# The first MLP product as Strassen's seven block products, with weight sums formed by accumulating DMA transfers

## The chip, the core and the metric

The kernel runs on one core of a Trainium2 chip. The metric is device time in microseconds, the median of several executions. A second number, the span, is the time from the first to the last instruction of one profiled execution; the rows further down come from that execution.

## The reference

Two decoder layers over 256 tokens of 2048 features. Each has a token mixer (differential attention in layer 0, dilated attention in layer 1), four heads that attend to 256 memory tokens, an output projection, and an MLP with 8192 hidden features. All in float32.

```
for i in range(DEPTH):                       # DEPTH = 2
    h = _rmsnorm(x, g_attn[i])
    proj = h @ w_in[i]                       # q, k, v, qm
    ...
    x = x + merged @ w_out[i]
    hm = _rmsnorm(x, g_mlp[i])
    x = x + jnp.square(jax.nn.relu(hm @ w_mlp1[i])) @ w_mlp2[i]
return _rmsnorm(x, g_final)
```

`w_mlp1` is 2048 x 8192, `w_mlp2` is 8192 x 2048. The change touches `hm @ w_mlp1[i]`.

## The kernel before

**Products.** A float32 number is held as two parts, hi and lo, in the type that TensorE takes at full rate; a product is hi x hi + hi x lo + lo x hi. Weights come from DRAM as float32 into a tile `raw`; `split` makes the parts: ScalarE copies to hi (line 108), VectorE subtracts to get lo (line 109). There are three raw tiles of 2048 columns, and four hi and four lo tiles of 1024.

**Two forms of matrix product.** `gemm_feat` (lines 124 to 151) keeps the weights stationary: per row tile of 128 and per block of 128 output features one matmul of 512 columns, hi weights against hi and lo activations side by side (line 142), and one of 256 columns, lo weights against hi activations (line 139). `gemm_tok_piece` (lines 153 to 163) keeps the tokens stationary, with three matmuls of 512 columns per row tile and token block (lines 161 to 163).

**The MLP.** It runs over 8 chunks of 1024 hidden features in each layer. `mlp_up(c)` does four `gemm_feat` with 2048 rows each (PSUM tile ps_u, weights hi_u and lo_u), adds the two halves (fb_u on line 214, ft_u on 216), squares the positive part (usq, line 540) and splits it into the tiles hT, hidden features by tokens. `mlp_down(c)` does four column blocks of 512 (PSUM tile psd, weights hi_d and lo_d), and adds each to x with the factor 1/rms^2 (line 562). The program is written as up(0), then for every c up(c+1), down(c).

**What sets the order.** The tile framework sorts the instructions when the program is built and fixes one list per engine; an engine takes its list in order. Two PSUM tiles of two banks (tag mm) hold what `gemm_feat` and the token form add up, four tiles of one bank (tag at) the rest. GpSimd does a few small operations and issues no transfer; loads are issued by SyncE.

```
split(hi, lo, raw[:, h * 1024:(h + 1) * 1024])
high(start=(k == 0), stop=False)
low(start=False, stop=False)
```

Of the kernel before, what the change touches and what calls it, by code (L numbers as in the profile page):

```python
# [9 lines left out]
F32 = mybir.dt.float32  # L10
F32R = mybir.dt.float32r
# [21 lines left out]
TMP = 6  # L33
GROUPS = ((128, 1), (512, 4), (2048, 16))
# [17 lines left out]
def trunk(ctx: ExitStack, tc: tile.TileContext, x, mem, g_attn, w_in, w_out, lambda_qk,  # L52
# [6 lines left out]
    apool = ctx.enter_context(tc.tile_pool(name="apool", bufs=8))  # L59
# [6 lines left out]
    x_sb = const.tile([P, 2, D], F32, name="x_sb")  # L66

    def load_weights(src, k, c, nm, parts=1):
        raw = wpool.tile([P, 2048], F32, tag="raw", name=f"raw_{nm}")
        n = k // parts  # L70
        for h in range(parts):
            yield nc.sync.dma_start(
                raw[:, h * n * c:(h + 1) * n * c].rearrange("p (k c) -> p k c", c=c),
                src[h * n * P:(h + 1) * n * P, :].rearrange("(k p) c -> p k c", p=P))
        yield raw
# [3 lines left out]
    first = [load_weights(w_in[0][pc * 1024:(pc + 1) * 1024, 3 * MIXW:3 * MIXW + 256], 8, 256, f"qm00_{pc}", 2)  # L79
             for pc in range(2)]  # L80
    for c in range(4):
        sl = slice(c * 512, (c + 1) * 512)
        nc.sync.dma_start(x_sb[:, :, sl], x[0].rearrange("(t p) d -> p t d", p=P)[:, :, sl])
        next(first[c // 2])
    first_raw = [next(f) for f in first]

# [6 lines left out]
    # matmuls on zeros that bring the tensor engine to its full clock while the first loads run  # L93
    zero = const.tile([P, 512], BF16, name="zero")
# [16 lines left out]
    def weights(src, k, c, nm, raw=None):  # L111
        """k row tiles of c columns, k * c = 2048, as two (hi, lo) pairs of k/2 row tiles."""
        if raw is None:
            *_, raw = load_weights(src, k, c, nm)
        res = []
        for h in range(2):
            hi = wpool.tile([P, 1024], F32R, tag="whi", bufs=4, name=f"hi_{nm}_{h}")
            lo = wpool.tile([P, 1024], F32R, tag="wlo", bufs=4, name=f"lo_{nm}_{h}")
            split(hi, lo, raw[:, h * 1024:(h + 1) * 1024])
            for kk in range(k // 2):  # L120
                res.append((hi[:, kk * c:(kk + 1) * c], lo[:, kk * c:(kk + 1) * c]))
        return res

    def gemm_feat(w, acts, nm, raws=(None, None)):
        """[256 features, 256 tokens] as [128, 2, 2, 256]: the two halves of dim 2 add up."""
        ps = pmm.tile([P, 2, 512], F32, tag="mm", name=f"ps_{nm}")
        k0 = 0
        for pc in range(2):
            wt = weights(w[pc * 1024:(pc + 1) * 1024, :], 8, 256, f"{nm}_{pc}", raws[pc])
            for kk in range(8):  # L130
                k = k0 + kk
# [18 lines left out]
            k0 += 8  # L150
        return ps.rearrange("p j (h t) -> p j h t", h=2)

    def gemm_tok_piece(ps, w, acts4, first, last, nm):
        """adds w[512, 512] against four activation tiles into ps [128, 2 token blocks, 512]."""
        wt = weights(w, 4, 512, nm)
        for kk in range(4):
            hi, lo = wt[kk]
# [10 lines left out]
    def to_feat(src_of_tok, c, dst, gcol, nm):  # L168
        """tokens x 512 features (chunk c) -> features x tokens times g, split into dst."""
# [14 lines left out]

    def sumsq(src, acc):
        junk = work.tile([P, 512], F32, tag="ev", bufs=EV, name="junk")
        nc.scalar.activation(junk[:, :src.shape[-1]], src, AF.Square, accum_out=acc)
# [6 lines left out]
    def rstd_of(ssq, nm):  # L194
        """ssq [128, 2, 4] -> 1 / rms by token [128, 2]."""
# [6 lines left out]
    def bcast_row(r, nm):  # L202
        """[128, 2] by token -> [128, 256], the tokens along the free axis in every partition."""
# [7 lines left out]
    def feat_sum(ps, nm):  # L211
        """the two halves of a gemm_feat result added: [128, 2, 256] in SBUF."""
# [20 lines left out]
    kmT = const.tile([P, DEPTH, NM, S], F32, name="kmT")  # L233
    vm = const.tile([P, DEPTH, 2, MEMW], F32, name="vm")
    memT = []
    mssq = small.tile([P, 2, 4], F32, tag="ssq", name="mssq")

    def load_mem(hf):
        m_t = wpool.tile([P, 2, 1024], F32, tag="raw", name=f"mem{hf}")
        nc.sync.dma_start(m_t, mem[0].rearrange("(t p) d -> p t d", p=P)[:, :, hf * 1024:(hf + 1) * 1024])  # L240
        for cc in range(2):
            c = 2 * hf + cc
            mt = act_tile(f"memT{c}")
            to_feat(lambda t: m_t[:, t, :], cc, mt, 4 * KT + 4 * (c - cc), f"mem{c}")
            memT.append(mt)
            for t in range(2):
                sumsq(m_t[:, t, cc * 512:(cc + 1) * 512], mssq[:, t, c:c + 1])

    def project_mem():
        mrstd = rstd_of(mssq, "mem")  # L250
        mrowb = bcast_row(mrstd, "mem")
        for i in range(DEPTH):
            for c in range(2):
                ps = gemm_feat(w_mem_kv[i][:, c * 256:(c + 1) * 256], memT, f"km{i}{c}")
                feat_scaled(kmT[:, i, 2 * c:2 * c + 2, :], ps, 1.0, mrowb, f"km{i}{c}")
# [4 lines left out]
            for t in range(2):  # L260
                nc.scalar.activation(vm[:, i, t, :], ps[:, t, :], AF.Copy, scale=mrstd[:, t:t + 1])

# [61 lines left out]
    def mem_head(i, h, qT, dst):  # L324
        """one memory head; dst [128, 2, 256] takes its output, features x tokens, split."""
        nm = f"m{i}{h}"
        sc = pat.tile([P, 2, S], F32, tag="at", name=f"sc_{nm}")
        for q in range(2):
            nc.tensor.matmul(sc[:, q, :], qT[:, q * P:(q + 1) * P], kmT[:, i, h, :], start=True, stop=True)
# [17 lines left out]
        for kb in range(2):  # L347
            nc.tensor.matmul(o[:, :S], vm[:, i, kb, h * HD:(h + 1) * HD], pT[:, kb, :],
# [301 lines left out]
```

## Time and profile before

| | us |
|---|---|
| median of 3 runs | 2239.72 |
| lowest, highest | 2239.68, 2239.79 |
| span of the profiled execution | 2237.8 |

The time of the profiled execution is not listed apart from its span; the span stands 1.9 us below the median. Of the span, TensorE is busy for 2226.3 us, VectorE for 1335.5, ScalarE for 1040.7, GpSimd for 14.0. The page of the profile gives such totals, the chain of work that ended last, groups of instructions by line (ps_u is the PSUM tile of the first MLP product, psd that of the second), and DMA issues with the time from issue to landing. Numbers behind a tile's name are buffer numbers.

### The profile page before, as it was taken

To read this page: it belongs to the slowest core of one execution; us is meant where nothing else is said; L and a number is where in the kernel's file an instruction comes from. 1 tells how busy PE (TensorE), PEld (TensorE's weight loads), DVE (VectorE), ACT (ScalarE), POOL (GpSimd) and SP (SyncE) were. 2 spreads that over 40 slices of the span, in tenths; PEclk is the share of its full clock that TensorE was granted. 3 is DMA by queue.
4 is the path that set the end of the run, shared out by engine and by line. 5 is a ranking of instruction groups with operands and counts; after the bars stand their busy time and mean duration, and the time that the engine had idled before them with its cause. 6 is when DMAs were issued, how large, how long until landed. Compare 5 with 4: busy or idle time off the path is not lost.

```text
span 2237.8 us, 27970 instructions
## 1 busy us (share of the span) xinstructions
PE 2226.3 (99%) x11462; PEld 1885.6 (84%) x11462; DVE 1335.5 (60%) x1568; ACT 1040.7 (47%) x1362; POOL 14.0 (1%) x26
## 2 busy tenths in 40 slices
PE   9999999999999999999999999999999999999998
PEld 7888878888888888888888888888888888888887
DVE  7557765565555555555666665555656555555555
ACT  7445554544344444444455544454444444434443
POOL 0000000000000000000000000000000000000000
PEclk9999999999999999999999999999999999999999
DMA  8554454566656656666555455456665665665664
GB/s 266 189 178 161 151 169 162 177 187 188 190 188 188 193 186 192 192 189 193 191 187 166 156 170 188 151 188 188 188 189 188 188 188 190 187 195 188 188 203 148
DMA packets 304849, 411.96 MB, mean 184 GB/s; under 512 B 6529, under 2 KB 203346, under 8 KB 304722
## 3 DMA queue, kind: packets, MB, share of 16 engines
q1 hardware_dynamic: 304448, 410.02, 57.7%
q8 instruction: 89, 1.46, 0.3%
q14 instruction: 38, 0.31, 0.0%
q10 hardware_dynamic: 274, 0.17, 0.0%
HBM read 408.07 MB, written 2.10 MB: 183 GB/s over the span
## 4 chain that ended last, share of the span: by engine, by line
PE 98%; DMA 1%; ACT 0%; issue 0%; DVE 0%; SPq 0%; POOL 0%; POOLq 0%; DVEq 0%
PE ps_u L142 21%; PE ps_u L139 11%; PE psd L163 10%; PE psd L162 10%; PE psd L161 10%; PE ps_q L142 4%; PE ps_k L142 4%; PE pso L163 3%; PE pso L161 3%; PE pso L162 3%; PE ps_q L139 2%; PE ps_k L139 2%; PE psv L163 2%; PE psv L162 2%; PE psv L161 2%; PE ps_km L142 1%
## 5 line engine op out<-in xcount | busy, mean ns | idle before, releaser
L142 PE MATMUL ps_u<-xTm,hi_u 128*128 128x512 f32 x2048 | 720.3, 398 | 0.0
L139 PE MATMUL ps_u<-xTm,lo_u 128*128 128x256 f32 x2048 | 564.9, 281 | 0.0
L142 PEld LDWEIGHTS ps_u<-xTm,hi_u 128*128 128x128 f32 x2048 | 381.5, 188 | 89.3
L109 DVE TENSOR_TENSOR lo_u<-raw_u,hi_u 128x1024 fp32r<-128x1024 f32 x256 | 313.1, 1224 | 232.3 <-ACT hi_u L108 230.4
L109 DVE TENSOR_TENSOR lo_d<-raw_d,hi_d 128x1024 fp32r<-128x1024 f32 x252 | 308.3, 1223 | 235.7 <-ACT hi_d L108 233.5
L108 ACT ACTIVATE hi_d<-raw_d 128x1024 fp32r<-128x1024 f32 x252 | 267.3, 1061 | 347.7 <-PE psd L163 293.2
L108 ACT ACTIVATE hi_u<-raw_u 128x1024 fp32r<-128x1024 f32 x256 | 271.1, 1059 | 286.9 <-PE ps_u L142 188.8
L163 PE MATMUL psd<-hi_d,hT 128*128 128x512 f32 x1008 | 392.6, 389 | 0.0
L161 PE MATMUL psd<-hi_d,hT 128*128 128x512 f32 x1008 | 392.4, 389 | 0.0
L162 PE MATMUL psd<-lo_d,hT 128*128 128x512 f32 x1008 | 392.3, 389 | 0.0
L139 PEld LDWEIGHTS ps_u<-xTm,lo_u 128*128 128x128 f32 x2048 | 386.7, 189 | 5.9
L162 PEld LDWEIGHTS psd<-lo_d,hT 128*128 128x128 f32 x1008 | 189.2, 188 | 39.4
L163 PEld LDWEIGHTS psd<-hi_d,hT 128*128 128x128 f32 x1008 | 189.2, 188 | 39.3
L161 PEld LDWEIGHTS psd<-hi_d,hT 128*128 128x128 f32 x1008 | 189.2, 188 | 38.8
L142 PE MATMUL ps_q<-xT,hi_q 128*128 128x512 f32 x384 | 138.0, 399 | 0.0
L142 PE MATMUL ps_k<-xT,hi_k 128*128 128x512 f32 x384 | 136.7, 395 | 0.0
L139 PE MATMUL ps_k<-xT,lo_k 128*128 128x256 f32 x384 | 108.2, 287 | 0.0
L139 PE MATMUL ps_q<-xT,lo_q 128*128 128x256 f32 x384 | 107.9, 286 | 0.0
L562 DVE SCALAR_TENSOR_TENSOR x_sb<-psd,rsq,x_sb 128x512 f32<-128x512 f32 x126 | 88.8, 746 | 24.4 <-PE psd L163 24.4
L214 ACT ACTIVATE fb_u<-ps_u 128x512 f32<-128x512 f32 x64 | 38.3, 598 | 119.0 <-PE ps_u L142 119.0
L216 DVE TENSOR_TENSOR ft_u<-ps_u,fb_u 128x512 f32<-128x512 f32 x64 | 44.3, 692 | 78.8 <-ACT fb_u L214 78.8
L109 DVE TENSOR_TENSOR lo_v<-raw_v,hi_v 128x1024 fp32r<-128x1024 f32 x48 | 58.8, 1225 | 49.7 <-ACT hi_v L108 49.6
(272 smaller groups left out, 2767.2 us busy)
## 6 DMA issues: line engine op xcount, KB each, us to landing
raw_u<-in_w_mlp_dram SPq DMA_DIRECT2D x128, 1024.0 KB, 5.7
raw_d<-in_w_mlp_dram SPq DMA_DIRECT2D x126, 1024.0 KB, 5.1
raw_q<-in_w_in_dram SPq DMA_DIRECT2D x24, 1024.0 KB, 5.2
raw_k<-in_w_in_dram SPq DMA_DIRECT2D x24, 1024.0 KB, 5.1
raw_v<-in_w_in_dram SPq DMA_DIRECT2D x24, 1024.0 KB, 5.0
raw_o<-in_w_out_dram SPq DMA_DIRECT2D x24, 1024.0 KB, 5.1
raw_km<-in_w_mem_kv_dram SPq DMA_DIRECT2D x8, 1024.0 KB, 5.3
raw_vm<-in_w_mem_kv_dram SPq DMA_DIRECT2D x8, 1024.0 KB, 5.0
```

The lines of the kernel that those rows point to most:

```text
L108: nc.scalar.activation(dst_hi, src, AF.Copy)
L109: nc.vector.tensor_tensor(dst_lo, src, dst_hi.bitcast(F32), op=ALU.subtract)
L139: nc.tensor.matmul(ps[:, j, 0:256], lo[:, cols], a[:, 0, :], **f)
L142: nc.tensor.matmul(ps[:, j, :], hi[:, cols], a.rearrange("p h t -> p (h t)"), **f)
L161: nc.tensor.matmul(ps[:, t, :], ah, hi, start=first and kk == 0, stop=False)
L162: nc.tensor.matmul(ps[:, t, :], ah, lo, start=False, stop=False)
L163: nc.tensor.matmul(ps[:, t, :], al, hi, start=False, stop=last and kk == 3)
L214: nc.scalar.activation(b, ps[:, :, 1, :], AF.Copy)
L216: nc.vector.tensor_tensor(t, ps[:, :, 0, :], b, op=ALU.add)
L562: nc.vector.scalar_tensor_tensor(xc[:, t, :], ps[:, t, :], rsq[:, t:t + 1], xc[:, t, :], op0=ALU.mult, op1=ALU.add)
```

## The change

The first MLP product takes another form. Pairs of row tiles (k = 2 kp and 2 kp + 1), the two token blocks, and the two halves of a chunk's 1024 columns are the 2 x 2 blocks of Strassen's scheme (in Winograd's variant). It needs seven products of sums in place of eight. `to_comb` makes the activation sums once in a layer (tiles cb_p1 to cb_p7, from 128 x 128 transposes). `up_weights` makes the weight sums for each pair and chunk: b takes the blocks (0,0) and (1,1) by one load, o the block (1,0) by another, both issued by SyncE; then three transfers issued by GpSimd add further blocks into b. Between them b is split into parts: b (bh, bl), s (sh, sl), t and v.

```
+    def up_weights(w, kp, f0, nm):
...
+        b = upool.tile([P, 2, 512], F32, tag="ux", bufs=UX, name=f"b_{nm}")
+        nc.sync.dma_start(b, bass.AP(tensor=w.tensor, offset=w.offset + 2 * kp * P * DFF + f0,
+                                     ap=[[DFF, P], [P * DFF + 512, 2], [1, 512]]))
+        o = upool.tile([P, 1, 512], F32, tag="ut", bufs=UT, name=f"o_{nm}")
+        nc.sync.dma_start(o, block(1, 0))
+        b11, b22 = pieces(b, "b")
+        p2 = piece(o[:, 0], "o")
+        nc.gpsimd.dma_start(b, block(0, 1, 2), accum_op=ALU.add)
+        t1, t3 = pieces(b, "s")
+        nc.gpsimd.dma_start(b[:, 0:1], block(1, 1), accum_op=ALU.add)
+        t2 = piece(b[:, 0], "t")
+        nc.gpsimd.dma_start(b[:, 0:1], block(1, 0), accum_op=ALU.add)
+        t4 = piece(b[:, 0], "v")
+        return {"p1": b11, "p2": p2, "p3": b22, "p5": t1, "p7": t3, "p6": t2, "p4": t4}
...
+        def product(ps, n, kp, hi, lo, last):
+            ah, al = comb[n][:, kp, 0, :], comb[n][:, kp, 1, :]
+            nc.tensor.matmul(ps, ah, hi, start=kp == 0, stop=False)
+            nc.tensor.matmul(ps, ah, lo, start=False, stop=False)
+            nc.tensor.matmul(ps, al, hi, start=False, stop=last)
...
         def mlp_up(c):
...
+            p12 = pmm.tile([P, 2, 512], F32, tag="mm", name=f"p12_{nm}")
+            p57 = pmm.tile([P, 2, 512], F32, tag="mm", name=f"p57_{nm}")
+            p3, p6, p4 = (pat.tile([P, 512], F32, tag="at", name=f"{n}_{nm}") for n in ("p3", "p6", "p4"))
...
+            for s in range(KP + 2):
+                if s < KP:
+                    wt[s] = up_weights(w_mlp1[i], s, f0, f"{nm}{s}")
+                for lag, names in ((0, ("p1", "p3", "p2")), (1, ("p5", "p7")), (2, ("p6", "p4"))):
+                    if 0 <= s - lag < KP:
+                        for n in names:
+                            product(bank[n], n, s - lag, *wt[s - lag][n], s - lag == KP - 1)
...
+            nc.vector.tensor_tensor(u2, c1, p6, op=ALU.subtract)
+            nc.vector.tensor_tensor(u4, u2, bank["p5"], op=ALU.add)
+            nc.vector.tensor_tensor(u3, u2, bank["p7"], op=ALU.add)
+            nc.vector.tensor_tensor(m22, u3, bank["p5"], op=ALU.add)
+            nc.vector.tensor_tensor(c21, u3, p4, op=ALU.add)
+            nc.vector.tensor_tensor(m12, u4, c3, op=ALU.add)
```

The seven sums come out as tokens by hidden features; `to_hT` transposes them on TensorE (16 transposes a chunk) and splits them into hT, as part of the down-projection before. Five b tiles (UX), three o tiles (UT) and seven tiles of 1024 columns (UP) for the parts serve the whole kernel. To make room, raw tiles shrink to 1024 columns (loads of 512 KB instead of 1024), hi and lo tiles go from four to three, one layer's memory keys and values wait in DRAM, and the distance tables are made in each layer.

On ScalarE, in the middle of an up-projection, this stood before: one copy for each 1024 columns of weights (hi_u), and the results of the block before in between (fb_u, hT).

```order
L108 ACTIVATE hi_u_0_0_5878<-raw_u_0_5876 128x1024
L108 ACTIVATE hi_u_0_1_5882<-raw_u_0_5876 128x1024
L108 ACTIVATE hi_u_1_0_5920<-raw_u_1_5918 128x1024
L214 ACTIVATE fb_u_5867<-ps_u_5782 128x512
L108 ACTIVATE hi_u_1_1_5924<-raw_u_1_5918 128x1024
```

The same engine there now, one pair of row tiles and the start of the next:

```order
L111 ACTIVATE bh_5622<-b_5618 128x1024
L111 ACTIVATE o_5626<-o_5620 128x512
L111 ACTIVATE sh_5630<-b_5618 128x1024
L111 ACTIVATE t_5635<-b_5618 128x512
L111 ACTIVATE v_5639<-b_5618 128x512
L111 ACTIVATE bh_5667<-b_5663 128x1024
L111 ACTIVATE o_5671<-o_5665 128x512
```

Four copies read the same tile b, each behind another transfer into it, and the next pair's first copy stands behind the last.

On GpSimd, around the MLP of layer 0, there stood only the small powers of the norms (L192), with no transfer:

```order
L192 TENSOR_TENSOR ro_3279<-v,nhalf 128x4
L192 TENSOR_TENSOR ro_3304<-v,nhalf 128x4
L192 TENSOR_TENSOR ro_3328<-v,nhalf 128x4
L192 TENSOR_TENSOR rstd_m_3991<-v,nhalf 128x2
L192 TENSOR_TENSOR rstd_a_9356<-v,nhalf 128x2
```

Now it holds, for the same two pairs as above, the accumulating transfers:

```order
L230 DMA b_5618<-in_w_mlp_dram 128x2x512
L232 DMA b_5618<-in_w_mlp_dram 128x512
L234 DMA b_5618<-in_w_mlp_dram 128x512
L230 DMA b_5663<-in_w_mlp_dram 128x2x512
L232 DMA b_5663<-in_w_mlp_dram 128x512
L234 DMA b_5663<-in_w_mlp_dram 128x512
```

All three of a pair come before the first of the next.

On VectorE, where an up-projection ends and a down-projection runs, this stood before (weight subtractions lo_d, the two steps of the last result, the two additions to x):

```order
L216 TENSOR_TENSOR ft_u_6056<-ps_u_5969,fb_u_6054 128x512
L540 SCALAR_TENSOR_TENSOR usq_6058<-ft_u_6056 128x512
L109 TENSOR_TENSOR lo_d_1_6104<-raw_d_6097,hi_d_1_6103 128x1024
L109 TENSOR_TENSOR hT_5960<-usq_6058,hT_5960 128x2x256
L109 TENSOR_TENSOR lo_d_0_6137<-raw_d_6134,hi_d_0_6136 128x1024
```

And this stands there now, from the last v of a chunk; t_02 are u2, u4 and u3 of the code, u_02_5758 is m22, p_02_5407 holds the banks of p5 and p7:

```order
L112 TENSOR_TENSOR v_5729<-b_5708,v_5729 128x512
L112 TENSOR_TENSOR bl_6137<-b_6132,bh_6136 128x1024
L639 TENSOR_TENSOR t_02_5782<-c_02_5753,p_02_5409 128x512
L112 TENSOR_TENSOR lo_d_5910<-raw_d_5907,hi_d_5909 128x1024
L112 TENSOR_TENSOR o_6140<-o_6134,o_6140 128x512
L640 TENSOR_TENSOR t_02_5784<-t_02_5782,p_02_5407 128x512
L641 TENSOR_TENSOR t_02_5783<-t_02_5782,p_02_5407 128x512
L683 SCALAR_TENSOR_TENSOR x_sb<-psd_5799,rsq_4261,x_sb 128x512 x2
L112 TENSOR_TENSOR lo_d_5928<-raw_d_5925,hi_d_5927 128x1024
L112 TENSOR_TENSOR hT_5797<-pu_5874,hT_5797 128x4x128
L642 TENSOR_TENSOR u_02_5758<-t_02_5783,p_02_5407 128x512
```

The last reader of the banks of p5 and p7 stands ten rows behind the last v; the second column block of the down-projection takes those banks next.

## Rows read from the trace of the kernel before

**Rows 1.** Totals of the page: busy time, share of span, instructions by engine.
```profile
span 2237.8 us, 27970 instructions
PE 2226.3 (99%) x11462; PEld 1885.6 (84%) x11462; DVE 1335.5 (60%) x1568; ACT 1040.7 (47%) x1362; POOL 14.0 (1%) x26
```

**Rows 2.** The chain that ended last, its shares of the span by line.
```profile
by line: PE ps_u L142 21.4%; PE ps_u L139 10.8%; PE psd L163 10.2%; PE psd L162 10.2%; PE psd L161 10.2%; PE ps_q L142 4.0%; PE ps_k L142 4.0%; PE pso L163 2.6%; PE pso L161 2.6%; PE pso L162 2.6%; PE ps_q L139 2.1%; PE ps_k L139 2.0%; PE p
```

**Rows 3.** Costliest groups: line, engine, tiles, shapes, count; busy us, mean ns; idle before.
```profile
L142 PE MATMUL ps_u<-xTm,hi_u 128*128 128x512 f32 x2048 | 720.3, 398 | 0.0
L139 PE MATMUL ps_u<-xTm,lo_u 128*128 128x256 f32 x2048 | 564.9, 281 | 0.0
L109 DVE TENSOR_TENSOR lo_u<-raw_u,hi_u 128x1024 fp32r<-128x1024 f32 x256 | 313.1, 1224 | 232.3 <-ACT hi_u L108 230.4
...
L108 ACT ACTIVATE hi_u<-raw_u 128x1024 fp32r<-128x1024 f32 x256 | 271.1, 1059 | 286.9 <-PE ps_u L142 188.8
L163 PE MATMUL psd<-hi_d,hT 128*128 128x512 f32 x1008 | 392.6, 389 | 0.0
...
L562 DVE SCALAR_TENSOR_TENSOR x_sb<-psd,rsq,x_sb 128x512 f32<-128x512 f32 x126 | 88.8, 746 | 24.4 <-PE psd L163 24.4
```

**Rows 4.** Groups by line and shape: operations of 512 columns.
```profile
L216 DVE TENSOR_TENSOR ft_u<-ps_u,fb_u 128x512 f32<-128x512 f32 x64 | 44.3, 692 | 78.8 <-ACT fb_u L214 78.8
L109 DVE TENSOR_TENSOR hT<-usq,hT 128x512 fp32r<-128x512 f32 x64 | 43.8, 685 | 0.0
L108 ACT ACTIVATE hT<-usq 128x512 fp32r<-128x512 f32 x64 | 40.5, 632 | 33.3 <-DVE usq L540 33.3
```

**Rows 5.** DMA queues (packets, MB, share); issues (count, KB each, us to landing).
```profile
q1 hardware_dynamic: 304448, 410.02, 57.7%
...
q10 hardware_dynamic: 274, 0.17, 0.0%
...
raw_u<-in_w_mlp_dram SPq DMA_DIRECT2D x128, 1024.0 KB, 5.7
raw_d<-in_w_mlp_dram SPq DMA_DIRECT2D x126, 1024.0 KB, 5.1
...
out_dram<-ot SPq DMA_DIRECT2D x8, 256.0 KB, 2.4
```

**Rows 6.** Timeline in a down-projection: start us, us, engine, line, operation, wait before.
```profile
646.40 0.39 PE L162 MATMUL psd<-lo_d,hT 128*128 128x512 f32 x1
...
646.43 1.06 ACT L108 ACTIVATE hi_d<-raw_d 128x1024 fp32r<-128x1024 f32 x1 [1.67 <-PE psd L163]
646.63 0.39 PE L163 MATMUL psd<-hi_d,hT 128*128 128x512 f32 x1
...
647.53 1.23 DVE L109 TENSOR_TENSOR lo_d<-raw_d,hi_d 128x1024 fp32r<-128x1024 f32 x1 [1.51 <-ACT hi_d L108]
```

**Rows 7.** Stretches: length, busy us (count) by engine, clock, DMA share, GB/s.
```profile
0.00:5.00 5.00, 3.81 (x9) 1.34 (x10) 3.40 (x10) 1.28 (x1) 3.12 (x13) 1.00 0.53 140
10.00:15.00 5.00, 3.94 (x25) 3.47 (x26) 4.48 (x12) 5.00 (x14) 0.00 (x0) 1.00 1.08 365
600.00:700.00 100.00, 100.00 (x513) 85.10 (x512) 58.78 (x60) 43.78 (x46) 0.00 (x0) 1.00 0.61 188
```

**Rows 8.** The chain in order of time: transposes of the memory tokens.
```profile
32.94 1.50 PE pt_mem L175 x12
```

**Rows 9.** Waits: who waited for whom, us in total, times, longest.
```profile
DVE lo_u L109 <- ACT hi_u L108: 230.4, 154, 1.6
ACT hi_u L108 <- PE ps_u L142: 188.8, 110, 1.8
```

More of the change, by code (lines that the diff above doesn't have):

```diff
@@ L33 @@
 TMP = 6
+KP = KT // 2
+UX = 5
+UT = 3
+UP = 7
+RAW = 3
+WH = 3
+PRODUCTS = ("p1", "p2", "p3", "p4", "p5", "p6", "p7")
 GROUPS = ((128, 1), (512, 4), (2048, 16))
@@ L83, in trunk @@
         nc.sync.dma_start(x_sb[:, :, sl], x[0].rearrange("(t p) d -> p t d", p=P)[:, :, sl])
-        next(first[c // 2])
-    first_raw = [next(f) for f in first]
+        first_raw.append(load_weights(w_in[0][sl, 3 * MIXW:3 * MIXW + 256], 4, 256, f"qm00_{c}"))
     ident = const.tile([P, P], F32, name="ident")
@@ L91, in trunk @@
     nc.gpsimd.memset(nhalf, -0.5)
-    zero = const.tile([P, 512], BF16, name="zero")
+    zero = work.tile([P, 512], BF16, tag="tmp", bufs=TMP, name="zero")
     nc.vector.memset(zero, 0.0)
@@ new lines, in up_weights, with block, pieces, piece @@
+    def up_weights(w, kp, f0, nm):
+        def block(k, n, times=1):
+            return bass.AP(tensor=w.tensor, offset=w.offset + (2 * kp + k) * P * DFF + f0 + n * 512,
+                           ap=[[DFF, P], [0, times], [1, 512]])
+        def pieces(a, m):
+            hi = upool.tile([P, a.shape[1], 512], F32R, tag="up", bufs=UP, name=f"{m}h_{nm}")
+            lo = upool.tile([P, a.shape[1], 512], F32R, tag="up", bufs=UP, name=f"{m}l_{nm}")
+            split(hi, lo, a)
+            return [(hi[:, n], lo[:, n]) for n in range(a.shape[1])]
+        def piece(a, m):
+            hl = upool.tile([P, 2, 512], F32R, tag="up", bufs=UP, name=f"{m}_{nm}")
+            split(hl[:, 0], hl[:, 1], a)
+            return hl[:, 0], hl[:, 1]
+        b = upool.tile([P, 2, 512], F32, tag="ux", bufs=UX, name=f"b_{nm}")
[12 more added lines that the diff above has]
+        return {"p1": b11, "p2": p2, "p3": b22, "p5": t1, "p7": t3, "p6": t2, "p4": t4}
@@ L529, in trunk @@
         hT = {}
[L531 to L541 removed]
+        ublk = {}
@@ L543, in trunk, with to_hT @@
+        def to_hT(c, n):
+            u, t, f = ublk[c][n]
+            pt = pat.tile([P, 4, P], F32, tag="at", name=f"pu_{i}{c}{n}")
+            for k in range(4):
+                nc.tensor.transpose(pt[:, k], u[:, k * P:(k + 1) * P], ident)
+            cols = slice(t * P, (t + 1) * P)
+            split(hT[c, f][:, :, 0, cols], hT[c, f][:, :, 1, cols], pt)
         final = i == DEPTH - 1
@@ L576, in trunk @@
         mlp_up(0)
+        for n in range(4):
+            to_hT(0, n)
         for c in range(NC):
```

207 lines of the change are left out of this document (123 added, 84 removed).

## The prediction

> **What bounds the kernel now.** Read the totals first: TensorE is busy for 99% of the span, VectorE 60%, ScalarE 47%, GpSimd 1% [rows 1]. Busy shares of a pipelined engine can flatter, so the second view is the chain of work that ended last: it runs through matmul lines, ps_u with 21.4 + 10.8 = 32.2% and psd with three times 10.2 = 30.6% [rows 2]. Third, the waits: where VectorE waits in the weight path it waits for ScalarE, and ScalarE waits for TensorE to give buffers back, never TensorE for either [rows 9]. So the time of before is the sum of matmul pitches. From the chain: ps_u is 0.322 x 2237.8 = 720.6 us for 2048 pairs of a 512- and a 256-column matmul [rows 3], 0.352 us a pair; psd is 684.8 us for 3 x 1008 matmuls of 512 columns, 0.2264 us each, which the start times in the timeline repeat (646.40, 646.63) [rows 6]. The remaining 832.4 us are attention, projections, start and end.
>
> **What the change takes off TensorE.** Per chunk of 1024 hidden features, 128 pairs become 7 products x 8 pairs of row tiles x 3 = 168 matmuls of 512 columns. At 0.2264 us, 16 chunks cost 2688 x 0.2264 = 608.6 us against 720.6: 112 us less. It adds 16 transposes a chunk; 12 took 1.50 us [rows 8], so 256 cost 32 us. If TensorE stayed the bound, the span would be 2237.8 - 112 + 32 = 2158 us.
>
> **What it adds in front of TensorE.** Work that was one copy and one subtraction per 1024 columns becomes a ladder for each pair of row tiles: split b, then an accumulating transfer into b, split again, transfer, split, transfer, split. Each rung needs the one before, because all four stand in the same tile. That alone would be hidden if several ladders were in flight; the order decides. On ScalarE the five copies of a pair stand as bh, o, sh, t, v, and only then bh of the next pair; I went through the whole order, and it is so at all 127 places where one pair follows another. On GpSimd the three transfers of a pair stand together in all 128 cases. An engine takes its instructions in order, so a copy that waits for a transfer holds back the next pair's first copy, and the ladder of one pair follows that of another without overlap.
>
> **The length of one ladder.** Copies of 1024 columns take 1.06 us on ScalarE and subtractions 1.22 on VectorE [rows 3]; of 512 columns 0.63 and 0.69 [rows 4]. On the path lie bh 1.06, bl 1.22, sh 1.06, sl 1.22, t 0.63 + 0.69, v 0.63 (the o split and the subtraction of v lie beside it): 6.5 us. A hand-over is short: the copy that starts at 646.43 ends at 647.49, the subtraction starts at 647.53 [rows 6]; six hand-overs add 0.2, so 6.7 us. To this come three landings, one of 512 KB and two of 256 KB.
>
> **The price of a landing.** No accumulating transfer and none from GpSimd's queue stands in the trace (only hardware queues do [rows 5]). The nearest rows: 1024 KB land in 5.1 us, 256 KB in 2.4 [rows 5], hence about 1.5 us fixed and 3.5 us per 1024 KB; 512 KB then take 3.3. Below bound: as quick as plain ones, 3.3 + 2.4 + 2.4 = 8.1. Above bound: twice that, 16.2, since the tile must be read as well and an engine issues them that issued none before. I take the bytes twice (3.5 and twice 1.8) and 2.0 us fixed for each: 5.5 + 3.8 + 3.8 = 13.1, an estimate from those rows. A free landing (0) is worked out too, because it can be no less.
>
> The Trainium skill (DMA: Bandwidth & Descriptors, section "Anatomy of one DMA — SWDGE (gpsimd) path") fits plain GpSimd transfers with 2.0 us plus bytes at 436 GB/s. That gives 3.2 + 2.6 + 2.6 = 8.4, an estimate from that page; it agrees with the lower bound and says nothing of accumulating. By it the time would be about 3210 us.
>
> **The sum.** Let L be the three landings and T = 6.7 + L: 19.8 us, against 21 x 0.2264 = 4.8 us of matmuls that one ladder feeds. What surrounds the ladders decides how many count. Of an up-projection that follows a down-projection, the order puts pair 0 and the start of pair 1 beside the down-projection of the chunk before, and the tail of pair 7 beside the next one's first column block. Left in between:
> (i) rest of pair 1, 4.2 + two small landings 7.6 = 11.8; pairs 2 to 6, 5 x 19.8 = 99.0; bh and bl of pair 7, 2.3: 113.1 us.
> (ii) the tail: L + 1.06 + 1.22 + 2 x (0.63 + 0.69) = 18.0 us until v of pair 7 is split; beside it TensorE has 48 + 21 matmuls, 15.6 us, so the ladder is later. Then TensorE needs the PSUM banks of p5 and p7 back. On VectorE the last reader stands behind bl of the next chunk, two weight subtractions, o, three sums, two residual adds and one hidden-tile split: 3 x 1.22 + 2 x 0.75 + 6 x 0.69 (the last reader among the six) = 9.3 us [rows 3, 4]. Together 27.3.
> (iii) column blocks 1 to 3 with the early matmuls of the next chunk: 159 x 0.2264 + 12 transposes 1.5 = 37.5.
> A period is thus 178 us, where before had 128 x 0.352 + 192 x 0.2264 = 88.5. In a layer, the first two up-projections follow on each other (11.8 + 13 T + 2.3 = 271.5), then come six times (i) = 678.6, seven times (ii) + (iii) = 453.6, and a last down-projection of 192 x 0.2264 = 43.5: 1447 us. Two layers less the 48 matmuls that the end keeps elsewhere (10.9) plus 832.4 give 3716 us. The median of before, 2239.7, is 1.9 us above the span of the profiled execution [rows 1]; the forecast is 3718.
> The same with L = 8.1: (i) 85.3, (ii) 15.6 + about 6.7, layer 1178, total 3177. With L = 16.2: (i) 130.6, (ii) 30.4, layer 1616, total 4054. One microsecond of L is worth some 109 us.
>
> **Edits costed at nothing.** Weight loads of 512 KB instead of 1024, with smaller rings: one feeds 12 matmuls, 2.7 us, while it lands in 3.3 with three in flight. The combinations of the activations: 8 pairs a layer, some 13 more small VectorE and ScalarE operations each, beside the output projection where VectorE is busy about 60%; the last two pairs can stand bare, 5 us a layer. Moving one layer's memory keys through DRAM and the distance tables built twice: beside matmuls, a few us. DMA volume: 1.75 times the bytes in the first product, 1792 KB per 19.8 us, half of the 188 GB/s that a quiet stretch moves now [rows 7].
>
> **Rivals.**
> *Ladders overlap and TensorE stays the bound* (faster): 2158 us. This decides if a ladder costs less than 4.8 us a pair. Against it: its copies and subtractions alone take 6.7. With L = 0 the sums are (i) 40.0, (ii) 15.6, layer 749, total 2319, still 3.5% above before. For it only the five b tiles, which the order does not use. 0.02.
> *Landings like plain loads* (L up to 9): 3177 to 3280. For it: free DMA engines. Against: the tile is read as well as written. 0.17.
> *Landings slow beyond the bound*: with L = 24, T = 30.7, total about 4900. For it: nothing in the trace measures the adding in the transfer. 0.13.
> *The clock.* In every row it was granted at 1.00, 2.4 GHz, even where TensorE was busy 3.8 of 5 us [rows 7]. In (i) it would be busy 4.8 of 19.8 us. At 1.2 GHz the ladder still covers 9.5 us of matmuls, but the 69 of the tail take 31.2 instead of 18.0: up to 13 us in each of 14 tails, 185 us, total up to 3900. 0.13.
> The Trainium skill (TensorE: Matmul & The Clock Gate, Part 1) says that the low clock is the default and activity lifts it, which speaks for this one; no stretch of this trace shows it.
>
> **How the numbers follow.** Forecast 0.54; the rivals as given; 0.01 remains for a break-even by chance. Range 3150 to 4250: it takes in the quick landings, the doubled ones and the clock, and leaves out the slow landings, the overlap and the break-even, 0.16. Faster by over 0.2% 0.02, within 0.2% (about what a measurement of this kernel can tell) 0.01, slower 0.97.
>
> **What would show it.** Right: the chain of waits passes from matmuls to transfers on b and the splits; TensorE's busy share falls to some 60%; in the up stretches bh follows bh by about 20 us; landings of b are listed at 3 to 6 us; TensorE waits for VectorE once after each down-projection's first block. Wrong: bh to bh below 10 us, or ScalarE's wait before sh near zero, or TensorE above 90% busy.

## The result, and the profile after

The changed kernel takes 4145.4 us (median of four executions, 4139.1 to 4147.1) against 2239.7 of before (2239.3 to 2239.8): a ratio of 1.850, 95% interval 1.848 to 1.853. The forecast of 3718 had the sign and the mechanism, and the range of 3150 to 4250 holds the result; the sum was 427 us short.

The totals of the changed kernel's page, with the row of TensorE's granted clock in 40 slices (tenths of full speed), answer to [rows 1]:

```profile
span 4137.2 us, 29282 instructions
...
PE 2779.6 (67%) x10310; PEld 2032.4 (49%) x10310; DVE 1589.3 (38%) x2082; ACT 1311.9 (32%) x1954; POOL 398.3 (10%) x418
...
PEclk9999855676767676767799996558585858585859
```

TensorE has 1152 matmuls less than before and is busy for only 67% of the span, and no other engine is busier. In the group that the page now lists first, in the place of ps_u in [rows 3], TensorE waits longer than it works. These are groups of the page: busy us, mean ns of one, then the idle time of that engine ahead of them and who ended it.

```profile
L604 PE MATMUL p<-sh,cb_p 128*128 128x512 f32 x256 | 167.9, 656 | 488.8 <-ACT sh L111 449.7
L159 PE MATMUL psd<-hi_d,hT 128*128 128x512 f32 x1008 | 409.8, 407 | 78.3 <-DVE x_sb L683 58.8
L112 DVE TENSOR_TENSOR sl<-b,sh 128x1024 fp32r<-128x1024 f32 x128 | 156.8, 1225 | 771.7 <-ACT sh L111 771.7
...
L111 ACT ACTIVATE sh<-b 128x1024 fp32r<-128x1024 f32 x128 | 135.3, 1057 | 848.5 <-DMA b<-in_w_mlp_dram 829.4
...
L111 ACT ACTIVATE t<-b 128x512 fp32r<-128x512 f32 x128 | 80.6, 629 | 654.7 <-DMA b<-in_w_mlp_dram 641.4
L111 ACT ACTIVATE v<-b 128x512 fp32r<-128x512 f32 x128 | 80.6, 629 | 649.5 <-DMA b<-in_w_mlp_dram 649.5
```

Read them from the last up: ScalarE sat idle for 848.5 + 654.7 + 649.5 = 2153 us ahead of three kinds of copies, and 2120 us of that were ended by a transfer into b. VectorE waits for ScalarE's copy, TensorE for the same copy. In [rows 9] the direction was the other one: ScalarE waited for TensorE.

One whole ladder, from the timeline of the changed kernel (start, length in us, engine, line, operation, wait ahead of it). Lines 230, 232 and 234 are the three accumulating transfers; the split of o and the subtractions of o and v, beside the path, are left out:

```profile
1091.15 1.04 ACT L111 ACTIVATE bh<-b 128x1024 fp32r<-128x1024 f32 x1
...
1092.22 1.22 DVE L112 TENSOR_TENSOR bl<-b,bh 128x1024 fp32r<-128x1024 f32 x1 [0.26 <-ACT bh L111]
...
1093.85 1.21 POOL L230 DMA_DIRECT2D b<-in_w_mlp_dram  x1 [6.79 <-DVE bl L112]
1100.39 1.06 ACT L111 ACTIVATE sh<-b 128x1024 fp32r<-128x1024 f32 x1 [7.68 <-DMA b<-in_w_mlp_dram]
1101.48 1.23 DVE L112 TENSOR_TENSOR sl<-b,sh 128x1024 fp32r<-128x1024 f32 x1 [7.43 <-ACT sh L111]
1103.11 0.89 POOL L232 DMA_DIRECT2D b<-in_w_mlp_dram  x1 [8.05 <-DVE sl L112]
1107.60 0.63 ACT L111 ACTIVATE t<-b 128x512 fp32r<-128x512 f32 x1 [6.16 <-DMA b<-in_w_mlp_dram]
1108.26 0.69 DVE L112 TENSOR_TENSOR t<-b,t 128x512 fp32r<-128x512 f32 x1 [5.56 <-ACT t L111]
1109.37 0.85 POOL L234 DMA_DIRECT2D b<-in_w_mlp_dram  x1 [5.37 <-DVE t L112]
1113.61 0.63 ACT L111 ACTIVATE v<-b 128x512 fp32r<-128x512 f32 x1 [5.38 <-DMA b<-in_w_mlp_dram]
1114.14 1.04 ACT L111 ACTIVATE bh<-b 128x1024 fp32r<-128x1024 f32 x1
```

From bh to the next bh are 22.99 us, and no split and no accumulating transfer of the next pair lies inside. Over 64 pairs in the middle of the up-projections the medians are: bh to first transfer 2.70, landing 6.63, split and hand-over 2.72, landing 4.39, split and hand-over 1.76, landing 4.34, v to bh 0.54; T is 23.1 (22.4 to 23.8). A landing is counted here from the start of the issue to the copy that reads the tile. The issues on the page, with the time to landing, and the two busy queues beside those of [rows 5]:

```profile
q1 hardware_dynamic: 229472, 378.59, 30.0%
q0 software_dynamic: 71680, 134.24, 21.0%
...
raw_d<-in_w_mlp_dram SPq DMA_DIRECT2D x252, 512.0 KB, 4.5
b<-in_w_mlp_dram SPq DMA_DIRECT2D x128, 512.0 KB, 3.7
b<-in_w_mlp_dram POOLq DMA_DIRECT2D x128, 512.0 KB, 6.5
b<-in_w_mlp_dram POOLq DMA_DIRECT2D x256, 256.0 KB, 4.3
o<-in_w_mlp_dram SPq DMA_DIRECT2D x128, 256.0 KB, 3.6
```

Three stretches of one period (length, then busy us and count of PE, PEld, DVE, ACT and POOL, granted clock, DMA share, GB/s): the end of the wait and the start of a down-projection's second column block, more of the second block, and an up stretch.

```profile
1034.00:1042.00 8.00, 6.42 (x20) 5.13 (x21) 6.25 (x10) 4.71 (x8) 0.90 (x1) 0.64 0.76 217
1042.00:1052.00 10.00, 10.00 (x52) 8.29 (x51) 7.01 (x8) 4.36 (x7) 0.87 (x1) 1.00 0.81 189
1078.00:1190.00 112.00, 54.88 (x111) 33.14 (x111) 25.78 (x29) 19.73 (x26) 14.81 (x15) 0.59 0.44 88
```

The period that begins with bh at 1028.38 is 202.3 us long; the other regular ones of both layers are 201 to 207. What stands ahead of layer 0's output projection takes what it took: its first matmul starts at 365.5, against 364.6 before.

### The profile page after: what moved, and what is told of

Same layout as the page of the kernel before. It is cut to its first block, busy times and chain, and to the rows that moved or that the text cites. A ratio compares the mean times of both kernels' runs of the same rounds, so it can differ in the third digit from the quotient of the medians.

```text
span 4137.2 us, 29282 instructions
## 1 busy us (share of the span) xinstructions
PE 2779.6 (67%) x10310; PEld 2032.4 (49%) x10310; DVE 1589.3 (38%) x2082; ACT 1311.9 (32%) x1954; POOL 398.3 (10%) x418
## 3 DMA queue, kind: packets, MB, share of 16 engines
q0 software_dynamic: 71680, 134.24, 21.0%
## 5 line engine op out<-in xcount | busy, mean ns | idle before, releaser
L604 PE MATMUL p<-sh,cb_p 128*128 128x512 f32 x256 | 167.9, 656 | 488.8 <-ACT sh L111 449.7
L112 DVE TENSOR_TENSOR sl<-b,sh 128x1024 fp32r<-128x1024 f32 x128 | 156.8, 1225 | 771.7 <-ACT sh L111 771.7
L111 ACT ACTIVATE sh<-b 128x1024 fp32r<-128x1024 f32 x128 | 135.3, 1057 | 848.5 <-DMA b<-in_w_mlp_dram 829.4
L604 PE MATMUL p<-v,cb_p 128*128 128x512 f32 x128 | 91.6, 716 | 436.1 <-ACT v L111 436.1
L112 DVE TENSOR_TENSOR v<-b,v 128x512 fp32r<-128x512 f32 x128 | 88.6, 692 | 605.2 <-ACT v L111 605.2
L112 DVE TENSOR_TENSOR t<-b,t 128x512 fp32r<-128x512 f32 x128 | 88.6, 692 | 566.7 <-ACT t L111 566.6
L230 POOL DMA_DIRECT2D b<-in_w_mlp_dram x128 | 154.3, 1205 | 1404.1 <-DVE bl L112 777.3
L111 ACT ACTIVATE t<-b 128x512 fp32r<-128x512 f32 x128 | 80.6, 629 | 654.7 <-DMA b<-in_w_mlp_dram 641.4
L111 ACT ACTIVATE v<-b 128x512 fp32r<-128x512 f32 x128 | 80.6, 629 | 649.5 <-DMA b<-in_w_mlp_dram 649.5
L604 PE MATMUL p<-t,cb_p 128*128 128x512 f32 x128 | 88.9, 694 | 278.4 <-ACT t L111 278.3
L232 POOL DMA_DIRECT2D b<-in_w_mlp_dram x128 | 116.1, 907 | 1091.4 <-DVE sl L112 1076.2
```

The source lines that it names most:

```text
L111: nc.scalar.activation(dst_hi, src, AF.Copy)
L112: nc.vector.tensor_tensor(dst_lo, src, dst_hi.bitcast(F32), op=ALU.subtract)
L230: nc.gpsimd.dma_start(b, block(0, 1, 2), accum_op=ALU.add)
L232: nc.gpsimd.dma_start(b[:, 0:1], block(1, 1), accum_op=ALU.add)
L604: nc.tensor.matmul(ps, ah, hi, start=kp == 0, stop=False)
```

## The experiments

Except for the changed kernel each time is one execution beside one of the kernel before (2239.5 to 2240.0). The executions of the changed kernel differ by 8 us; the differences that are read below are 19 us or more.

**e1_plain: what does the adding cost?** The transfers write instead of add.

```
-        nc.gpsimd.dma_start(b, block(0, 1, 2), accum_op=ALU.add)
+        nc.gpsimd.dma_start(b, block(0, 1, 2))
...
```

> The three GpSimd transfers of each pair write the block into b instead of adding it; sizes, order and waits stay, the weight sums are left out. Theory (three landings in series set the ladder, and adding is part of their price): landings from GpSimd's queue fall from 6.6, 4.4, 4.3 us to about 4.7, 3.6, 3.6, a ladder from 23.1 to about 19.7 us; at 109 us per us the time is about 3770 us. Rival (the price is that of the software queue, adding is free): landings, ladder and time stay within 2%, 4060 to 4220 us.

3697.9 us, T 19.9. The queue and the issues on its page:

```profile
q0 software_dynamic: 38912, 134.24, 11.5%
...
b<-in_w_mlp_dram POOLq DMA_DIRECT2D x128, 512.0 KB, 5.6
b<-in_w_mlp_dram POOLq DMA_DIRECT2D x256, 256.0 KB, 3.0
```

T is as expected, the time 72 us lower than the theory's 3770. The adding costs 447 us, 3.3 us a ladder. Most of the loss stays: plain transfers in the same order still leave the kernel 65% above before. So the adding makes the ladder longer, but it is a quarter of the loss of 1906 us.

**e3_two: is one rung a third of the landings?** The third transfer is left out.

```
-        nc.gpsimd.dma_start(b[:, 0:1], block(1, 0), accum_op=ALU.add)
```

> The third transfer of each pair is left out, v is split from the tile as t left it, so one sum is missing. Theory (ladders in series): from the start of t to the next bh 1.1 us instead of 6.6, a ladder 17.5 instead of 23.1 us; 86 ladders in the two layers, 14 rests of pair 1 and 14 tails (there at most 4.7) give 4137 less 622, about 3515 us. Rival (low clock or vector work carries the time): less than 200 us come off.

3595.6 us, T about 17.6: the ladder is as expected, the time 81 us above the theory's 3515. A rung less is 5.5 us less a ladder and 550 us in all, 100 us for each us of T; the forecast priced 109, and e1 gives 447 / 3.26 = 137. Why the two differ is not shown.

**e2_skew: does the order make it serial?** The same transfers; the program is written so that ladders of several pairs mix.

```
-            for s in range(KP + 2):
+            for s in range(KP + 3):
...
+                for lag, names in ((3, ("p4",)), (2, ("p6",)), (1, ("p5", "p7")), (0, ("p1", "p3", "p2"))):
+                    if 0 <= s - lag < KP:
+                        wt[s - lag][1][lag]()
```

> Same instructions, but the program is written so that the rungs of several pairs mix: on ScalarE v of two pairs back and t of one pair back now stand between bh and sh of a pair. Theory (the fixed order that lets one ladder follow another is the cause): the small landings go beside the large one, bh to bh falls from 23.1 to some 10.5 to 12 us, time 2900 to 3250 us. Rival (the transfers are slow because the DMA engines are full of adding traffic): landings stretch as they overlap, bh to bh stays above 17 us, time above 3550 us.

3089.9 us: 1055 us come from order alone. T is 13.3, above the theory's 12. The timeline of this kernel shows why (ScalarE, then GpSimd, where 242, 238 and 233 are the third, second and first transfer):

```profile
907.50 1.04 ACT L111 ACTIVATE bh<-b 128x1024 fp32r<-128x1024 f32 x1
...
913.52 0.63 ACT L111 ACTIVATE t<-b 128x512 fp32r<-128x512 f32 x1 [3.94 <-DMA b<-in_w_mlp_dram]
919.49 1.06 ACT L111 ACTIVATE sh<-b 128x1024 fp32r<-128x1024 f32 x1 [5.33 <-DMA b<-in_w_mlp_dram]
920.45 1.04 ACT L111 ACTIVATE bh<-b 128x1024 fp32r<-128x1024 f32 x1
...
909.27 0.87 POOL L238 DMA_DIRECT2D b<-in_w_mlp_dram  x1 [6.03 <-DVE sl L112]
910.40 1.21 POOL L233 DMA_DIRECT2D b<-in_w_mlp_dram  x1 [0.26 <-issue]
```

The scheduler placed sh of a pair ahead of bh of the next, so that one landing of the three still lies between them: bh to transfer 2.90, landing 9.33, sh to the next bh about 1.0 make up the 13.3. The landing is longer than the 6.63 of the serial kernel while two transfers lie beside each other.

**e15_skewplain: what is left in that order?** e2_skew with transfers that write.

> As e2_skew, with transfers that write instead of add (the sums are left out, the output is not the reference's). It completes a square: serial and accumulating 4145, serial and plain 3698, mixed order and accumulating 3090. Theory (in e2_skew the landings are long, 9.3, 4.3 and 6.7 us, since accumulating transfers that lie beside one another take turns at the DMA engines): the ladder falls from 13.3 to 8 to 10.5 us a pair, time 2480 to 2800. Rival (the mixed order has a ladder of its own, in which hand-overs and splits make the 13.3): ladder 12 or more, time above 2950.

2726.7 us, T 10.0, by the theory's figures. The rival has a part in it: T is again first rung, landing and sh, 2.89 + 6.10 + 1.0. The mixed order keeps a ladder of one landing, and adding lengthens that landing from 6.1 to 9.3. The four kernels make a square: serial 4145 and 3698, mixed 3090 and 2727 (adding, writing). Order is worth 1055 and 971 us, adding 447 and 363.

**e9_clock: does the low clock matter?** 62 more matmuls a pair, with a stationary tile of zeros, keep TensorE busy while it would wait.

```
+                            fill = {"p2": 22, "p7": 20, "p6": 20}.get(n, 0)
...
+                            for d in range(fill):
+                                nc.tensor.matmul(bank[n], zr, wt[s - lag][n][0], start=False,
```

> Computes all of the reference; the changed kernel with 62 more matmuls a pair whose stationary tile is zero (22 behind p2, 20 behind p7, 20 behind p6), so that TensorE is busy while it would wait for the ladder. Theory (the ladder of landings, splits and hand-overs sets the period, the lower granted clock is a result of TensorE's waiting and costs only the matmuls that stand outside the ladder): granted clock above 0.95 in the up-projection, ladder still 22.5 to 23.8 us a pair, time lower by 0 to 110 us: 4035 to 4145. Rival (the low clock lengthens the ladder or the matmuls set the time): time lower by more than 200 us, ladder below 21.5.

4457.7 us, a time outside both expectations; clock and ladder are the theory's. In its up stretch the clock is up:

```profile
1110.00:1250.00 140.00, 128.32 (x542) 102.86 (x541) 33.51 (x37) 27.04 (x33) 15.96 (x16) 0.98 0.45 95
```

T is 23.3 there, at 0.98, against 23.1 at 0.59 (a mean between the clock's two levels, 1.2 and 2.4 GHz): the ladder does not run on TensorE's clock. That part is settled. The total is not a measure of what the clock costs elsewhere, since the fillers stand in TensorE's list ahead of products and down-projections, and the period grew from 202 to 226.

**e4_dve: no transfer on the ladder.** The fourth block is loaded, and VectorE forms the sums.

```
+        nc.vector.tensor_tensor(b[:, 0], b[:, 0], no[:, 0], op=ALU.add)
+        nc.vector.tensor_tensor(t[:, 0], b[:, 0], b[:, 1], op=ALU.add)
+        nc.vector.tensor_tensor(b[:, 1], b[:, 1], no[:, 0], op=ALU.add)
+        nc.vector.tensor_tensor(no[:, 1], no[:, 1], t[:, 0], op=ALU.add)
```

> No accumulating transfer: the fourth block is loaded too (512 KB with o), and VectorE makes the sums by four additions of 512 columns in a pair. Theory (landings in the ladder are the loss, not Strassen's form): bh to bh falls to the ladder of splits and sums, 7.5 to 8.5 us with VectorE busy 7.3 of it, time 2350 to 2550 us. Rival (the extra splitting and the smaller tiles already cost most of it): bh to bh above 12 us, time above 2900 us.

2458.6 us, as expected: 41% less than the changed kernel, still 10% above before. T is 7.4, just below the expected 7.5, a period about 99. In the timeline VectorE has nine operations back to back from sl at 860.88 to the last sum, which ends at 867.69, and then waits briefly for the copy that reads the sums:

```profile
860.88 1.22 DVE L112 TENSOR_TENSOR sl<-b,sh 128x1024 fp32r<-128x1024 f32 x1 [0.58 <-ACT sh L111]
...
867.01 0.68 DVE L235 TENSOR_TENSOR no<-no,t 128x512 f32<-128x512 f32 x1
868.55 1.23 DVE L112 TENSOR_TENSOR sl<-b,sh 128x1024 fp32r<-128x1024 f32 x1 [0.86 <-ACT sh L111]
```

**e14_nosum: what does the rest of the change cost?** e4_dve without its four additions.

> As e4_dve, with the four additions of a pair left out: the seven products multiply weight blocks instead of sums, so the output is not the reference's. VectorE then has 4.5 us a pair (splits alone), TensorE 4.75. Theory (behind the ladder nothing of the change costs much; the sums are what Strassen's products cost here): TensorE sets the time, 2158 to 2230, which is the floor of the PE-bound rival. Rival (the order of loads, the buffers or the evictions of the seven products hold the up-projection back too): 2300 or more.

2176.8 us. The totals and one stretch of two periods (columns as above):

```profile
PE 2151.0 (99%) x10310; PEld 1786.3 (82%) x10310; DVE 1561.6 (72%) x2082; ACT 1317.0 (61%) x1954; POOL 19.5 (1%) x34
```

```profile
797.30:964.40 167.10, 167.10 (x753) 138.13 (x753) 130.01 (x151) 108.14 (x140) 0.00 (x0) 1.00 0.66 202
```

TensorE is the bound again, pairs follow each other in 4.76 us and periods in 83.5, against 88.5 before. So the seven products, transposes, smaller loads and buffers end 19 us above what the overlap rival said (2158). The sums eat the gain: formed on VectorE they cost 282 us.

**e5_pool and e6_skewpool: the additions on GpSimd.** e5_pool is e4_dve with `nc.gpsimd` in place of `nc.vector`; e6_skewpool writes the second half of a pair behind the first half of the next.

> Computes all of the reference. As e4_dve (the fourth block is loaded, the sums of weight blocks are formed by additions of 512 columns, no accumulating transfer), but the four additions of a pair are on GpSimd instead of VectorE: only the engine of the additions differs from e4_dve. Theory (the period is set by the serial ladder of a pair, and the additions are rungs of it): no run has shown the price of an addition of 512 columns on GpSimd; at the 0.63 to 0.69 us that VectorE took the time is e4_dve's 2458 or below, down to 2300, since VectorE is rid of 2.6 us a pair; at three times that (2 us each, two or three of them between the splits of b and of s) the ladder grows by some 3 us a pair, 8 pairs, 16 column groups: 2458 + 128 x 3 = 2840 at most. Rival (VectorE's load, not the ladder, sets e4_dve's time): below 2300 whatever an addition costs on GpSimd.

> Computes all of the reference. As e5_pool, and the program is written so that the second half of a pair (splits of s, t, v and their products) stands behind the first half of the next pair (b, o). Theory (a ladder in program order is what makes the period long): the additions on GpSimd lie beside the next pair's splits and leave the path, so the time is below e5_pool's by most of their price, 2200 to 2450, and TensorE's share of busy time is above e4_dve's 93%. Rival (buffers, not order, hold a pair back, since this kernel has the same number of them): within 3% of e5_pool.

2613.9 and 2613.4 us. The first is within the theory's bounds, and the rival, below 2300, fell: an addition takes about 1.3 us where VectorE is quiet and 1.3 to 1.7 in the mean of its four lines, and T is 9.15. The slowest and the quickest of the four lines:

```profile
L232 POOL TENSOR_TENSOR b<-b,no 128x512 f32<-128x512 f32 x128 | 214.5, 1676 | 1185.5 <-DVE bl L112 1023.9 <-ACT xs_xm L194 85.4 <-DVE tot_m L253 76.2
...
L235 POOL TENSOR_TENSOR no<-no,t 128x512 f32<-128x512 f32 x128 | 163.4, 1276 | 83.9 <-DVE o L112 83.9
```

The second tells nothing on the skew: written so, it gave ScalarE, VectorE and GpSimd the very order of e5_pool, and only its time repeats.

**e8_mix: two additions on each engine**, and eight buffers for split weights.

```
+            nc.vector.tensor_tensor(b[:, 0], b[:, 0], no[:, 0], op=ALU.add)
...
+            nc.gpsimd.tensor_tensor(t[:, 0], b[:, 0], b[:, 1], op=ALU.add)
+            nc.vector.tensor_tensor(b[:, 1], b[:, 1], no[:, 0], op=ALU.add)
+            nc.gpsimd.tensor_tensor(no[:, 1], no[:, 1], t[:, 0], op=ALU.add)
```

> Computes all of the reference. As e6_skewpool, with two of the four additions back on VectorE and one more buffer for split weights (8 instead of 7, paid for by one less temporary and one less raw tile). Theory: as e6_skewpool with shorter additions on GpSimd, 2180 to 2420. Rival (GpSimd and VectorE additions hinder each other, or buffers of the rest of the layer are now short): not below e6_skewpool.

2513.2 us: 100 below e6_skewpool, 55 above e4_dve, and so outside the theory (at most 2420) and the rival (not below e6_skewpool). The kernel changes the engines and the buffers together, so it does not say which.

**e10_gp3 and e13_up8: the sums of t and v beside the splits.** GpSimd forms them in a tile of their own, VectorE adds once over 1024 columns.

```
+        nc.gpsimd.tensor_tensor(t[:, 0], b[:, 0], b[:, 1], op=ALU.add)
+        b11, b22 = pieces(b, "b")
+        nc.gpsimd.tensor_tensor(t[:, 0], t[:, 0], no[:, 0], op=ALU.add)
+        nc.vector.tensor_tensor(b, b, no[:, 0:1].to_broadcast([P, 2, 512]), op=ALU.add)
+        p2 = piece(no[:, 1], "o")
+        nc.gpsimd.tensor_tensor(no[:, 1], no[:, 1], t[:, 0], op=ALU.add)
```

> Computes all of the reference. As e4_dve, with the sums cut to fit: the sum that p6 needs and the sum that p4 needs are formed on GpSimd from the loaded blocks in a tile of their own (three additions of 512 columns, from 1.3 to 1.7 us each in e5_pool: 4.0 to 4.8 a pair, beside the splits), and the two sums that p5 and p7 need in one VectorE addition of 1024 columns (about 1.2 us by the splits' subtractions of that size). VectorE then has some 5.8 us a pair, against 7.1 in e4_dve, and TensorE's matmuls 4.75. Theory (with no transfer on the ladder the up-projection runs at the load of VectorE, 7.5 us a pair in e4_dve): 5.8 to 6.3 us a pair, time 2458 - 128 x 1.2 to 1.7 = 2240 to 2310. Rival (the hand-overs of the ladder, not the load, make the 7.5): 2380 to 2460.

> Computes all of the reference. As e10_gp3 with eight buffers for split weights instead of seven (one temporary and one tile for sums less). Theory (VectorE's load sets the pace): within 2% of e10_gp3, a little below since more of the next column group is split ahead, 2200 to 2310. Rival (buffers hold a pair back): 3% or more below e10_gp3.

2605.8 and 2582.3 us: slower than e4_dve, outside the theory and the rival of e10_gp3. T is 8.6, not 5.8 to 6.3. e13_up8 is within 2% of e10_gp3, as its theory said, and far above its 2200 to 2310. The eighth buffer, with the two tiles given up for it, is worth 0.9%, so this exchange does not explain the miss. VectorE was to lose 1.3 us a pair, some 166 us in all; it is busy for 63 us more than in e4_dve. These are the totals of e4_dve and e10_gp3:

```profile
PE 2286.9 (93%) x10310; PEld 1822.3 (74%) x10310; DVE 1881.0 (77%) x2594; ACT 1293.0 (53%) x1954; POOL 20.6 (1%) x34
...
PE 2354.4 (90%) x10310; PEld 1856.6 (71%) x10310; DVE 1944.5 (75%) x2210; ACT 1302.8 (50%) x1954; POOL 669.5 (26%) x418
```

The operations themselves became longer. This is sl in e10_gp3 over all 128 pairs (least, median, most in ns, first and last start):

```profile
L112 DVE TENSOR_TENSOR sl<-b,sh x128: 1209/2270/2368, 382.5 to 2499.7; 128x1024 fp32r<-128x1024 f32 x128
```

In the same kernel's timeline, an addition on VectorE beside one on GpSimd, and one alone:

```profile
1008.49 1.29 POOL L232 TENSOR_TENSOR t<-t,no 128x512 f32<-128x512 f32 x1 [2.76 <-DMA no<-in_w_mlp_dram]
...
1008.54 2.32 DVE L233 TENSOR_TENSOR b<-b,no 128x1024 f32<-128x1024 f32 x1
...
1017.17 1.21 DVE L233 TENSOR_TENSOR b<-b,no 128x1024 f32<-128x1024 f32 x1
```

The same VectorE addition takes 1.21 us alone and 2.32 when GpSimd's began 0.05 us earlier: about its own time plus the other's 1.29. Which of the two started first decides. Of the 768 splits and additions on VectorE, 228 start while a GpSimd addition runs and take 1.07 us longer in the median; in 134 a GpSimd addition starts, and they take their usual time, while GpSimd's takes longer (1.60 in the median). Where the two meet, they cost about as much as one after the other, so a sum moved to GpSimd takes little load off VectorE there. That the longer operations are all of the 147 us above e4_dve isn't shown: GpSimd also waits for loads in this kernel. The Trainium skill (SBUF — State Buffer, section "Who interferes with whom") says that a VectorE instruction with two SBUF inputs contends with a GpSimd instruction that reads SBUF; these rows agree, 2.32 against 1.21.

No version here that computes all of the reference beats the kernel before. e4_dve keeps VectorE busy for 169.5 of 198 us, 84.8 a period, still below the 88.5 of before. So a gain is not excluded by load. It would want the additions of a pair spread over the down-projection, for which more split weights must be held; that is argued and was not tried, nor was an accumulating kernel in which no landing lies between two copies of ScalarE.

## Why the prediction was right, and where its sum was short

**What bounds the kernel, and the serial ladder: right, and shown.** The waits passed from matmuls to transfers and splits; five copies in the order of the list made bh follow bh by 23.1 us; TensorE waits once behind the first column block. e2_skew shows that order carries more than half of the loss (1055 of 1906 us). What was off in the sum is sizes: by the forecast's own 109 us for each us of the ladder, the 3.3 us by which T was short are worth 360 of the 427.

**Splits and hand-overs: 6.7 forecast, 7.7 measured.** The copies and subtractions had the durations of [rows 3] and [rows 4] to 0.01 us. The hand-overs were mis-sized: 0.04 us holds from ScalarE to VectorE. From VectorE to GpSimd it is 0.40: sl starts at 1101.48, takes 1.23, and the transfer starts at 1103.11. Three of them are 1.2 us where the sum had 0.1.

**The landings: 13.1 forecast, 15.4 measured,** between the bounds of 8.1 and 16.2: 6.6 + 4.4 + 4.3. Doubling the bytes was too little: by the page's 6.5 and 4.3, 256 KB more cost 2.2 us where the sum had 1.8. That leaves 2.1 as the fixed part, where it had 2.0; this split is an estimate, since the large transfer has another shape. The lower bound was wrong for GpSimd's queue: e1_plain, which has no adding, needs 5.9 + 3.1 + 3.1 = 12.1, not 8.1. One of the two rows behind it is no load: the 2.4 us are those of the stores out_dram<-ot [rows 5], and the load of o, 256 KB as well, lands in 3.6 in the changed kernel. GpSimd works on an issue for 0.85 to 1.21 us in the changed kernel, which no row of before could show. Together T is 23.1 for 19.8.

By the Trainium skill (DMA: Bandwidth & Descriptors, section "Anatomy of one DMA — SWDGE (gpsimd) path") the landings would have been 8.4, an estimate from its fit for plain transfers; the plain ones of e1_plain took 12.1, and the measurement decides.

**The period: 178 forecast, 202.3 in the one looked at.** (i) is 134.5 against 113.1: five ladders take 116.4 where the sum had 99.0, and the other 4.0 come from pair 1. Its first transfer starts at 1068.11 and sh only at 1076.93, while column block 3 ends at 1075.3, and its rest takes 14.2 for 11.8. (ii) is 28.1 against 27.3, but by another sum: the tail is 21.7, not 18.0, and the wait behind it 6.4, not 9.3, so that the near agreement is luck. The reason for the wait failed as well. These are the rows that end it:

```profile
1034.12 1.40 DVE L683 SCALAR_TENSOR_TENSOR x_sb<-psd,rsq,x_sb 128x512 f32<-128x512 f32 x2
...
1035.58 0.79 PE L159 MATMUL psd<-hi_d,hT 128*128 128x512 f32 x1 [5.31 <-DVE x_sb L683]
...
1037.17 0.68 DVE L642 TENSOR_TENSOR u<-t,p 128x512 f32<-128x512 f32 x1
```

The second column block waits for the first block's own addition to x, and it starts before m22 (L642), the last reader of the banks of p5 and p7. So it takes the first block's banks and not those of p5 and p7. (iii) is 39.7 against 37.5: behind the wait the first matmuls start 0.43 us apart and not 0.23, at a clock of 0.64 in the stretch from 1034, and that is 2.0 of the 2.2 us.

Summed from the trace over both layers, the first two up-projections (from sh of pair 1 on) take 316.4 and 315.2 us against 271.5, 89 more together. The twelve (i) are 275 more, the fourteen (ii) and (iii) only 18 (in two of them the wait is 1.4 us and not 6.4), layer 0's last down-projection 3. The rest is where the ladders begin, a term that the sum had at nothing: sh of pair 1 starts at 484.5, 23.5 us behind the end of the output projection of before (461.0), and in layer 1 it stands 361.7 us behind the last down-projection of layer 0, where before's output projection ended 344.7 behind it. In the lists of ScalarE and VectorE bh (465.70) and bl (475.96) of pair 1 stand among the activation sums and the last weight splits of the output projection. With 3 us more at the end, and 7 that the forecast's 832.4 had too much, this makes up the 421 us by which the span exceeds the sum's 3716.

**Rivals.** Overlap: fell; e14_nosum shows that its floor was sound (2177 for 2158), and e4_dve that the sums on VectorE hold it off even without a landing (T 7.4 where TensorE needs 4.8). Quick landings and slow landings: fell, 15.4 lies between. The clock: the mechanism is there, with 0.59 in the up stretch. That agrees with the Trainium skill (TensorE: Matmul & The Clock Gate, Part 1), by which activity lifts a clock that is low by default. The trace of before does show the low level, other than the prediction read. Its first 14 matmuls of 512 columns start 0.43 us apart; in the changed kernel the last of the same 14 are 0.22 apart. The 1.00 of the first stretch in [rows 7] stands there though no clock was recorded before 6.9 us. Behind TensorE's last matmul the clock is at 0.65, a mean over a stretch in which it fell:

```profile
1.19 5.97 PE L98 MATMUL pw<-zero 128*128 128x512 bf16 x14 [1.19 <-DVE zero L95]
...
2230.00:2237.80 7.80, 0.00 (x0) 0.00 (x0) 2.28 (x7) 1.70 (x4) 0.56 (x1) 0.65 0.71 269
```

The price of up to 185 us was too high. e9_clock shows that the ladder owes the clock nothing. In 13 of the 14 tails TensorE waited 1.6 to 2.8 us for v, so the ladder and not its own clock ended them. Behind the waits the matmuls at the low level cost 27 us in all 14 together.

**Edits costed at nothing:** right as a sum in e14_nosum, where they and the seven products together end 19 us above the PE-bound figure. In the changed kernel the ladders begin 23.5 and 17.0 us late, where 5 us a layer were allowed for the activation sums; that these sums are the whole delay is read from the order, and no run shows it alone.

## What to carry to other kernels

A chain of transfers into one tile, with work on the tile between them, costs the sum of its landings unless the engine lists let other chains in between, so read the list of the engine that waits before pricing durations: here order alone was worth 1055 us. Where an operation that the trace doesn't show sits on such a chain three times, price also who hands over to whom: here VectorE to GpSimd took ten times as long as ScalarE to VectorE. Before moving load to another engine, look whether the two can work at the same time.

## What the runs showed of the hardware

- An accumulating transfer of 512 KB landed in 6.5 us and one of 256 KB in 4.3; the same transfers without adding in 5.6 and 3.0. On the 16 DMA engines the 134 MB took 21.0% of 4137 us, 869 us, with adding, and 11.5% of 3696, 425 us, without: twice the time, with 71680 packets for 38912.
- GpSimd is busy for 0.85 to 1.21 us in the mean of the three lines with each accumulating issue, 380 us in all, and starts 0.40 us after the VectorE operation that it waits for.
- An addition of 1024 columns on VectorE took 2.32 us when one on GpSimd had begun 0.05 us earlier, alone 1.21. In e10_gp3 the operation that started second waited: 228 VectorE operations beside a running GpSimd addition took 1.07 us longer in the median, 134 in which one began took no longer.
- TensorE's granted clock fell to 0.59 where it was busy for 55 of 112 us, and stood at 0.98 where fillers kept it busy for 128 of 140. Behind a wait of 5.31 us the next matmuls of 512 columns started 0.43 us apart, then 0.23.
